# Two rooms instead of one for the value pairs of a mixer layer, each pair loaded one tile earlier

## The chip, the cores and the metric

The kernel runs on one core of one Trainium2 chip. The metric is the device time of one execution in microseconds (us); below 0.3% of it (about 3.8 us) a difference counts as none. The profile is one execution taken by the hardware profiler. Engines are named as in it: PE (matrix multiply), PEld (its weight loads), DVE (vector), ACT (scalar), POOL, and SP, which only issues transfers; "ACTq" and the like is the engine's sequencer, for instance when it issues a transfer (DMA).

## The reference

One layer over 1024 tokens of 1024 channels, in float32. What matters here:

```python
h = rmsnorm(x, g_pre_mix)
proj = h @ w_in                              # u_pool (512) | q (512) | k (512) | v (512)
y_pool = multiscale_pool(u_pool, ...) @ w_br_pool     # 4 groups, trailing means over 2, 4, 8, 16 tokens
o_sb = stick_breaking_attention(q, k, v)              # 8 heads of 64, strictly causal
gates = sigmoid(h @ w_gate + b_gate)
x = x + rmsnorm((g_pool * y_pool + g_sb * (o_sb @ w_br_sb)) @ w_out, g_post_mix)
h2 = rmsnorm(x, g_pre_mlp)
x = x + rmsnorm(relu(h2 @ w_up)**2 @ w_down, g_post_mlp)
```

The kernel's attention needs, in place of v, the difference of each token's v row and the next one's ("value pairs").

## The kernel before, in words

**Precision and tiling.** Each float32 matrix is split into a high and a low part, and each product is three matmuls (`mm3`, L110 to L112) of 128x128 by 128x512. The stages follow each other: input and v, then `phase_project` (q, k and gates), then attention, merge and MLP. The change touches only what runs beside `phase_project`.

**The products.** `phase_project` handles twelve pairs of column blocks (`PAIRS`, L499): pairs 0 to 4 are gates, 5 to 8 are q, k, q, k, and 9 to 11 gates. Each pair is seven half products (a Strassen scheme), numbered here c = 0 to 83, so that pair i has c = 7i to 7i+6; each is 12 matmuls into a PSUM bank. `newbank` (L666) deals seven banks out of three pools in turn: "d" (2 banks), "z" (2), "at" (3). So product c shares its bank with c+6 in the first two pools and with c+9 in the third; `later` takes four such banks too, all before c = 30. The bank is read by DVE or ACT into the parts u, c11, v and c22 (L693 to L717); u has two buffers, each other part one.

**The sixteen staged results.** Of a pair, products 2, 5, 6 and 7 complete the results c11, c22, v and u (L695, L712, L716, L718). For the gates a result is squashed in place and stored. For q and k (`result`, L548 to L558) it is split by ACT (L550) and DVE (L551) into a staged tile, which POOL's queue stores in two or four transfers of 256 KB (L556, and L558 for q alone). Call these S1 to S16: S1 to S4 are c11, c22, v and u of pair 5, and so on to S16, u of pair 8. Their tiles take turns between two rooms (`staged`, L537): S1 in m1, S2 in m0, S3 in m1 and so on, odd ones in m1, even ones in m0.

**The rooms.** Pool `mx` has four rooms m0 to m3 of 4 KB per partition, one buffer each: a new tile in a room waits until the one before it has been read and, if it is stored, until its store has landed.

**The background.** `later` (L560) is a generator. One step of it runs inside each product, before the product's own result is dealt with (L679), and a second one at twelve of the products 6 to 33 (L681). Its step numbers, from 0, are used below; from product 34 on, step s runs inside product c = s - 13, and so before the result of that product asks for its room.

- Steps 9 to 42: pooling of four groups g. Group g loads u (m0 or m3 in turn, L568), makes g+1 running sums in m1 and m2 in turn (L590), the difference (L595 to L599), its high and low parts ph and pq (L603, L604), the matmuls, two scaled results (L611, L612) that overwrite the last sum and u, and stores both to `yscr` (L619). For g = 3 the matmuls are in step 40 and the stores in step 41; pq is in m0, ph in m1, the last sum in m2, u in m3.
- Steps 43 to 84: eight value tiles t. Tile t loads its pair p on ACT's queue (two transfers, L626) in step 43, 49, 55, 61, 67, 73, 77, 81, and three steps later subtracts (DVE, L631), splits (ACT L634, DVE L635) into v, and stores v to `sscr` (POOL, L636). The room of p is m2, and of v m3; for t = 5 and 7 it is m0 and m1.

**Behind the stage** attention's first head is loaded into m2 and m3 (L724) and the second into m0 and m1 (L748, L781 to L787), both on SP's queue, with the second half of the pooling result behind the second head.

**The order on each engine** is made at compile time by a list scheduler: it takes a later instruction ahead of one whose operands or room it expects later. On the chip each engine then runs its list in that order.

Of the kernel before, what the change touches and what calls it, by code (L numbers as in the profile page):

```python
# [19 lines left out]
F32 = mybir.dt.float32  # L20
# [12 lines left out]
P = 128  # L33
H = 512
NK = 8
# [17 lines left out]
class Block:  # L53
# [506 lines left out]
    def later(self, newbank):  # L560

        nc = self.nc
        def whole(n, dt=F32, name="ps"):
            return self.mx.tile([P, 1024], dt, name=name, tag=f"m{n}")

        def u_load(g):
            u = whole(3 * (g % 2), name="u")
            nc.scalar.dma_start(u, self.uscr[g])  # L568
            return u

        nxt_u = u_load(0)
        wm = whole(1)[:, :512].rearrange("p (g n) -> p g n", g=4)
        nc.scalar.dma_start(wm, self.wmix)
        for _ in range(6):
            yield
        yield
        yield
        wmh, wml = (self.rp.tile([P, 4, P], F32R, name=f"wm{n}", tag=f"rb{n}") for n in range(2))
        nc.scalar.copy(wmh, wm)
        nc.vector.tensor_sub(wml, wm, wmh.bitcast(F32))  # L580
        yield
        for g in range(4):
            iu = 3 * (g % 2)
            u = nxt_u
            cur, n = u, 0
            for i in range(g + 1):
                sh = 1 << i
                n = 1 + i % 2
                nxt = whole(n, name="win")
                nc.vector.tensor_add(nxt[:, sh:], cur[:, sh:], cur[:, : 1024 - sh])  # L590
                nc.vector.tensor_copy(nxt[:, :sh], cur[:, :sh])
                cur = nxt
                yield
            w = 1 << (g + 1)
            nc.vector.scalar_tensor_tensor(  # L595
                out=cur[:, w:], in0=cur[:, w:], scalar=1.0 / w, in1=u[:, w:], op0=ALU.mult, op1=ALU.subtract
            )
            nc.vector.tensor_mul(cur[:, :w], cur[:, :w], self.rcnt[:, :w])
            nc.vector.tensor_sub(cur[:, :w], cur[:, :w], u[:, :w])  # L599
            yield  # L600
            sc = self.vt[:, V_PSC + g : V_PSC + g + 1]
            ph, pq = whole(3 - n, F32R, "ph"), whole(3 - iu, F32R, "pq")
            nc.scalar.copy(ph, cur)  # L603
            nc.vector.tensor_sub(pq, cur, ph.bitcast(F32))  # L604
            yield
            yield
            ds = [self.zps.tile([P, H], F32, name="dm", tag="o", bufs=1), newbank()]
            for h, d in enumerate(ds):
                c = slice(h * H, h * H + H)
                self.mm3(d, [(wmh[:, g, :], wml[:, g, :], ph[:, c], pq[:, c])])  # L610
                nc.scalar.activation(cur[:, c].bitcast(F32R), d, AF.Copy, scale=sc)  # L611
                nc.vector.scalar_tensor_tensor(  # L612
                    out=u[:, c].bitcast(F32R), in0=d, scalar=sc, in1=cur[:, c], op0=ALU.mult, op1=ALU.subtract
                )
            if g < 3:
                nxt_u = u_load(g + 1)
            yield
            for t, scr in zip((cur, u), self.yscr):
                nc.gpsimd.dma_start(scr[:, g, :], t)  # L619
            yield  # L620
            yield
        for t in range(NK):
            n = 0 if t in (5, 7) else 2
            p = self.mx.tile([P, 2, H], F32, name="vpair", tag=f"m{n}")
            for j in range(2):
                nc.scalar.dma_start(p[:, j, :], self.vscr[t * P + j : t * P + j + P, :])  # L626
            yield
            yield
            yield
            e = p[:, 0, :]  # L630
            nc.vector.tensor_sub(e, e, p[:, 1, :])  # L631
            e = e.rearrange("p (h x) -> p h x", h=8)
            v = self.mx.tile([P, 8, P], F32R, name="vs", tag=f"m{n + 1}")
            nc.scalar.copy(v[:, :, 0:64], e)  # L634
            nc.vector.tensor_sub(v[:, :, 64:128], e, v[:, :, 0:64].bitcast(F32))  # L635
            nc.gpsimd.dma_start(self.sscr[t], v.rearrange("p h x -> p (h x)").bitcast(F32))  # L636
            yield
            if t < 5:
                yield
                yield  # L640
# [1033 lines left out]
```

## Time and profile before

| | |
|---|---|
| median of 3 runs | 1263.16 us (1262.45 to 1266.2) |
| the profiled execution | 1262.18 us, span 1260.4 us, mean granted PE clock 0.998 |
| DVE, ACT, POOL busy | 77%, 50%, 14% of the span |
| `phase_project` in the trace | about 105 to 336 us from the span's start |
| DMA | 283.27 MB, 225 GB/s mean |

In the views quoted below a row of a timeline reads: start, duration, engine, line, operation, output<-inputs, shapes, count, and in square brackets how long the engine had been idle and what ended it. Rows of windows give the busy time of each engine (with its number of instructions), the granted clock ("PEclk", 1.00 is full) and the DMA share. A step of the chain of waits is start, duration, what.

### The profile page before, as it was taken

Reading aid. Unit: us, or ns where it says so; the run is one execution under the profiler, and the core shown is the slowest. Engines: PE = TensorE matmul, PEld = TensorE weight load, DVE = VectorE, ACT = ScalarE, POOL = GpSimd, SP = SyncE. Lnnn points to the kernel's source line nnn. Section 1 sums busy time; section 2 is a strip of 40 time slices with the busy share of each in tenths; the row PEclk is TensorE's granted clock in tenths of the full one; section 3 lists DMA queues with packets and bytes.
Section 4 is the critical chain, followed back from the end, with each engine's and each line's share of the span. In section 5 each row is a group of like instructions: output and inputs, shape, how many; then the busy total and the mean of one; then the engine's idle time right before and its main releaser. Section 6 shows DMA issues by size and latency. Waiting matters only on the chain.

```text
span 1260.4 us, 16197 instructions
## 1 busy us (share of the span) xinstructions
PE 1238.4 (98%) x5707; PEld 1021.2 (81%) x5707; DVE 968.6 (77%) x1311; ACT 631.9 (50%) x1010; POOL 180.0 (14%) x320
## 2 busy tenths in 40 slices
PE   9999999999999999999999999999999999999998
PEld 6887788788787887878788888888888888888887
DVE  8849886786488998778797879878854655776975
ACT  7237543344266576663566645554554433344352
POOL 2212111442001101110110012221121100001000
PEclk9999999999999999999999999999999999999999
DMA  6586896987998665446657577665559996557552
GB/s 225 168 232 177 241 275 155 317 298 240 320 358 334 204 184 150 101 137 215 225 161 242 195 268 264 235 224 200 183 198 340 300 305 228 185 194 252 202 190 68
DMA packets 110497, 283.27 MB, mean 225 GB/s; under 512 B 12496, under 2 KB 17744, under 8 KB 109264
## 3 DMA queue, kind: packets, MB, share of 16 engines
q1 hardware_dynamic: 65840, 165.41, 37.6%
q0 software_dynamic: 31040, 91.26, 25.2%
q10 hardware_dynamic: 13536, 25.57, 6.2%
q8 instruction: 45, 0.74, 0.2%
q14 instruction: 36, 0.29, 0.1%
HBM read 208.65 MB, written 94.50 MB: 241 GB/s over the span
## 4 chain that ended last, share of the span: by engine, by line
PE 72%; DMA 9%; issue 8%; DVE 7%; ACT 2%; POOL 1%; ACTq 0%; SPq 0%; DVEq 0%; POOLq 0%
PE d L112 17%; PE d L110 17%; PE d L111 17%; PE o L853 2%; PE dbr L108 2%; PE dbr L111 2%; PE dbr L112 2%; DMA qscr<-ks 2%; PE at L829 2%; DMA vpair<-vscr 1%; DVE T L816 1%; PE sw L110 1%; DMA vscr<-ev 1%; PE sw L112 1%; PE sw L111 1%
## 5 line engine op out<-in xcount | busy, mean ns | idle before, releaser
L111 PE MATMUL d<-blo,whi 128*128 128x512 f32 (+1 forms) x456 | 172.3, 378 | 0.0
L112 PE MATMUL d<-bhi,wlo 128*128 128x512 f32 (+1 forms) x456 | 171.9, 378 | 0.0
L110 PE MATMUL d<-bhi,whi 128*128 128x512 f32 (+1 forms) x456 | 168.7, 378 | 0.0
L112 PEld LDWEIGHTS d<-bhi,wlo 128*128 128x128 f32 x456 | 85.8, 188 | 16.1
L111 PEld LDWEIGHTS d<-blo,whi 128*128 128x128 f32 x456 | 85.7, 188 | 16.0
L110 PEld LDWEIGHTS d<-bhi,whi 128*128 128x128 f32 x456 | 85.5, 188 | 15.9
L816 DVE TENSOR_TENSOR_SCAN T<-T,past 128x512 f32<-128x512 f32 (+3 forms) x64 | 85.0, 1346 | 4.9 <-ACT T L814 4.5
L111 PE MATMUL d<-b_lo,whi 128*128 128x512 f32 x196 | 76.2, 390 | 0.5 <-DVE b_lo L1100 0.5
L110 PE MATMUL d<-b_hi,whi 128*128 128x512 f32 x196 | 75.7, 390 | 0.0
L112 PE MATMUL d<-b_hi,wlo 128*128 128x512 f32 x196 | 74.2, 389 | 0.0
L78 DVE TENSOR_TENSOR wlo<-wraw,whi 128x1024 fp32r<-128x1024 f32 x45 | 54.9, 1220 | 13.9 <-ACT whi L76 12.3
L76 ACT CAST whi<-wraw 128x1024 fp32r<-128x1024 f32 x45 | 47.5, 1055 | 36.0 <-PE d L111 20.1
L1395 ACT CAST whi<-slots_hi 128x1024 fp32r<-128x1024 f32 x29 | 30.5, 1053 | 68.8 <-PE d L111 62.6
L1397 DVE TENSOR_TENSOR wlo<-slots_hi,whi 128x1024 fp32r<-128x1024 f32 x29 | 35.5, 1224 | 38.2 <-ACT whi L1395 38.2
L814 ACT ACTIVATE T<-z 128x256 f32<-128x256 f32 (+2 forms) x96 | 45.2, 493 | 35.1 <-PE z L812 31.2
L1395 ACT CAST whi<-slots_lo 128x1024 fp32r<-128x1024 f32 x27 | 28.4, 1053 | 62.3 <-PE d L111 52.1
L110 PE MATMUL sw<-h_hi,whi 128*128 128x512 f32 x144 | 56.9, 395 | 2.1 <-DVE c L694 2.1
L111 PE MATMUL sw<-h_lo,whi 128*128 128x512 f32 x144 | 56.6, 393 | 0.0
L112 PE MATMUL sw<-h_hi,wlo 128*128 128x512 f32 x144 | 56.2, 393 | 0.0
L839 ACT CAST ahi<-at 128x512 fp32r<-128x512 f32 (+1 forms) x96 | 44.1, 484 | 22.3 <-PE at L829 20.0
L840 DVE TENSOR_TENSOR alo<-at,ahi 128x512 fp32r<-128x512 f32 (+1 forms) x96 | 49.9, 541 | 6.7 <-ACT ahi L839 6.6
L1397 DVE TENSOR_TENSOR wlo<-slots_lo,whi 128x1024 fp32r<-128x1024 f32 x27 | 33.0, 1222 | 26.0 <-ACT whi L1395 25.9
(438 smaller groups left out, 3444.9 us busy)
## 6 DMA issues: line engine op xcount, KB each, us to landing
wraw<-w SPq DMA_DIRECT2D x53, 512.0 KB, 4.9
ext_b<-ascr SPq DMA_DIRECT2D x40, 512.0 KB, 6.9
wscr<-w POOLq DMA_DIRECT2D x32, 512.0 KB, 9.4
slots_hi<-w SPq DMA_DIRECT2D x10, 1024.0 KB, 7.9
slots_lo<-w SPq DMA_DIRECT2D x10, 1024.0 KB, 8.8
qq<-qscr SPq DMA_DIRECT2D x32, 256.0 KB, 5.2
pscr<-p SPq DMA_DIRECT2D x32, 256.0 KB, 3.0
u<-pscr ACTq DMA_DIRECT2D x32, 256.0 KB, 4.5
```

Source lines behind the costliest of these rows:

```text
L76: nc.scalar.copy(hi, raw)
L78: self.lows.append(nc.vector.tensor_sub(lo, raw, hi.bitcast(F32)).ins)
L108: nc.tensor.matmul(ps, wh, rh, start=first and i == 0, stop=False)
L110: nc.tensor.matmul(ps, wh, rh, start=first and i == 0, stop=False)
L111: nc.tensor.matmul(ps, wh, rl, start=False, stop=False)
L112: self.last_mm = nc.tensor.matmul(ps, wl, rh, start=False, stop=last and i == n - 1).ins
L814: self.after = nc.scalar.activation(f, z[:, :n], AF.Sigmoid, scale=-1.0)
L816: nc.vector.tensor_tensor_scan(f[:, ::-1], f[:, ::-1], past[:, ::-1], 1.0, ALU.mult, ALU.max)
L839: self.att_hi = nc.scalar.copy(hi[:, c:], at[:, c:]).ins
L840: self.att_lo = nc.vector.tensor_sub(lo[:, c:], at[:, c:], hi[:, c:].bitcast(F32)).ins
L1395: last_split[0] = nc.scalar.copy(hi, src).ins
L1397: last_split[1] = nc.vector.tensor_sub(lo, src, hi.bitcast(F32)).ins
```

## The change

The value pairs t = 0, 2, 4, 6 use m2 and m3, and t = 1, 3, 5, 7 use m0 and m1. Each pair is loaded a tile ahead: the load of t = 0 moves to step 40, behind the last pooling matmuls, and the loads of t = 1 to 7 move to steps 44, 50, 56, 62, 68, 74 and 78; the subtraction, the split and the store stay in steps 46, 52, 58, 64, 70, 76, 80 and 84. In the pooling groups 0 and 3 the running sums begin in m2 instead of m1, so that the last sum of group 0 is in m2 and that of group 3 in m1, and their ph in the other one.

```diff
+        def v_load(t):
+            p = self.mx.tile([P, 2, H], F32, name="vpair", tag=f"m{2 - 2 * (t % 2)}")
+            for j in range(2):
+                nc.scalar.dma_start(p[:, j, :], self.vscr[t * P + j : t * P + j + P, :])
+            return p
...
-                n = 1 + i % 2
+                n = 1 + (i + (g in (0, 3))) % 2
...
             if g < 3:
                 nxt_u = u_load(g + 1)
+            else:
+                nxt_p = v_load(0)
             yield
...
         for t in range(NK):
-            n = 0 if t in (5, 7) else 2
-            p = self.mx.tile([P, 2, H], F32, name="vpair", tag=f"m{n}")
-            for j in range(2):
-                nc.scalar.dma_start(p[:, j, :], self.vscr[t * P + j : t * P + j + P, :])
+            n = 2 - 2 * (t % 2)
+            p = nxt_p
             yield
+            if t < NK - 1:
+                nxt_p = v_load(t + 1)
             yield
             yield
             e = p[:, 0, :]
```

## The prediction

> **What bounds the kernel now.** I read the page first, then PE's windows of 10 us, then the waits that ended PE's gaps there, then the lists of ACT and DVE between 200 and 320 us.
>
> ```profile
> span 1260.4 us, 16197 instructions
> ...
> PE 1238.4 (98%) x5707; PEld 1021.2 (81%) x5707; DVE 968.6 (77%) x1311; ACT 631.9 (50%) x1010; POOL 180.0 (14%) x320
> ```
>
> PE is busy 98% of the span, so a change can only pay where PE stops, and can only cost where it makes PE stop. Windows beside the background generator (columns: window, length, then busy time and count of PE, PEld, DVE, ACT, POOL, then clock, DMA share, GB/s):
>
> ```profile
> 180.00:190.00 10.00, 10.00 (x46) 8.29 (x45) 7.00 (x12) 4.08 (x7) 0.08 (x1) 1.00 0.67 257
> 210.00:220.00 10.00, 9.81 (x44) 7.81 (x43) 4.01 (x6) 4.56 (x6) 1.50 (x2) 1.00 1.10 289
> 220.00:230.00 10.00, 7.87 (x28) 6.04 (x27) 7.37 (x12) 1.82 (x3) 3.23 (x6) 0.83 0.82 276
> 230.00:240.00 10.00, 10.00 (x46) 8.29 (x45) 7.61 (x11) 3.79 (x6) 3.13 (x7) 1.00 1.01 358
> ```
>
> A full window holds 46 matmuls, so one matmul takes 0.22 us and a product (12 of them) 2.7 us. The window 220 to 230 holds 28: 18 are missing, 3.9 us, and 2 more in the window before, 0.4 us. The clock of 0.83 is (1 - 0.83) x 10 = 1.7 us of it, the rest is PE standing still. The chain of waits through that place, and PE's rows that ended a gap:
>
> ```profile
> 205.23 8.40 DMA yscr<-win
> ...
> 214.01 9.10 DMA vpair<-vscr
> ...
> 223.23 0.06 DVE vpair L631
> ...
> 223.84 0.69 DVE c L694
> ...
> 224.57 0.79 PE sw L110
> ```
>
> ```profile
> 218.73 0.50 PE L110 MATMUL sw<-h_hi,s1hi 128*128 128x512 f32 x1 [0.19 <-ACT u L693]
> ...
> 224.57 0.79 PE L110 MATMUL sw<-h_hi,whi 128*128 128x512 f32 x1 [2.13 <-DVE c L694]
> ```
>
> The store of the last pooling sum (room m2) takes 8.40 us; only then can the first value pair be loaded into m2, 9.10 us; DVE holds at its subtraction (L631); behind it in DVE's list stands the c11 of pair 5 (L694), and PE waits 2.13 us for that. The two gaps also show how far PE gets without DVE and ACT. The u and c11 of pair 5 are products 35 and 36, so PE stood at products 41 and 42, which share their banks: six products on.
>
> **How a room is handed on.** This decides the case. In m0 stand, by the program text before: pq of group 3, S2, S4 and so on to S12, then p of t = 5 (called p5, its split result v5), S14, S16, p7; in m1: ph, S1, S3 to S15, v5, v7.
>
> ```profile
> 203.98 0.68 ACT L611 ACTIVATE win<-sw,vt 128x512 fp32r<-128x512 f32 x1
> ...
> 229.41 0.63 ACT L550 ACTIVATE qs<-c 128x512 fp32r<-128x512 f32 x1 [4.23 <-DVE c L710]
> ```
>
> From 203.98, when the last pooling product is read and with it pq is done, to 229.41, when S2 is written, m0 is empty. p5 needs nothing but the room, for its data are old; its load is the row at 290.74 below. So a room is handed on in the order of the text, even if a later tenant is ready and the room empty. Here is what it costs when p5 then comes between S12 and S14 (ACT's list, then DVE's):
>
> ```profile
> 267.74 0.63 ACT L550 ACTIVATE qs<-c 128x512 fp32r<-128x512 f32 x1 [0.38 <-DMA qscr<-ks]
> 268.94 0.63 ACT L550 ACTIVATE qs<-c 128x512 fp32r<-128x512 f32 x1 [0.58 <-DMA qscr<-ks]
> ...
> 277.27 0.63 ACT L550 ACTIVATE qs<-v 128x512 fp32r<-128x512 f32 x1 [1.47 <-DMA qscr<-qs]
> ...
> 279.27 0.63 ACT L550 ACTIVATE qs<-u 128x512 fp32r<-128x512 f32 x1
> 288.29 0.63 ACT L550 ACTIVATE ks<-c 128x512 fp32r<-128x512 f32 x1 [8.39 <-DMA qscr<-qs]
> ...
> 290.74 1.08 ACTq L626 DMA_DIRECT2D vpair<-vscr  x2
> ...
> 294.99 0.63 ACT L550 ACTIVATE ks<-v 128x512 fp32r<-128x512 f32 x1 [0.98 <-DMA qscr<-ks]
> ...
> 301.64 0.62 ACT L634 CAST vs<-vpair 128x512 fp32r<-128x512 f32 x1 [5.07 <-DMA qscr<-ks]
> ...
> 303.02 0.63 ACT L550 ACTIVATE ks<-c 128x512 fp32r<-128x512 f32 x1 [0.23 <-DVE vs L635]
> ...
> 309.88 0.63 ACT L550 ACTIVATE ks<-u 128x512 fp32r<-128x512 f32 x1 [1.75 <-DMA qscr<-ks]
> ...
> 312.53 0.58 ACT L693 COPY u<-sw 128x512 f32<-128x512 f32 x1
> ...
> 316.01 0.81 ACTq L626 DMA_DIRECT2D vpair<-vscr  x2
> ```
>
> ```profile
> 280.12 0.69 DVE L710 TENSOR_TENSOR c<-v,sw 128x512 f32<-128x512 f32 x1
> ...
> 302.29 0.69 DVE L635 TENSOR_TENSOR vs<-vpair,vs 128x512 fp32r<-128x512 f32 x1 [2.96 <-ACT vs L634]
> ...
> 303.68 0.69 DVE L551 SCALAR_TENSOR_TENSOR ks<-c,ks 128x512 fp32r<-128x512 f32 x1
> ...
> 304.89 0.68 DVE L710 TENSOR_TENSOR c<-v,sw 128x512 f32<-128x512 f32 x1
> ```
>
> The rows are S9 (267.74), S10, S11, S12 (279.27), S13 (288.29), p5's load (290.74), S15 (294.99), v5 (301.64), S14 (303.02), S16 (309.88), the u of pair 10 (312.53), p7's load. S14 holds c22 of pair 8, complete at 280.12, and gets m0 only at 303.02, because p5 leaves m0 when v5 is split, and v5 must wait for S15's store in m1: 5.07 us of waiting on ACT. The next c22 (pair 9, L710 at 304.89) runs straight behind DVE's read of S14 (303.68): a staged result that waits keeps its part, and the part keeps a PSUM bank. PE doesn't feel it here. From the same rows a room is held 10.6 us by a q result (9.53, 10.33, 11.02, 11.47) and 6.6 us by a k result (6.70, 6.65, 6.86, 6.13).
>
> **The change part by part.**
>
> *First pair early.* In step 40 its room m2 holds ph of group 3, free at 203.98. Its load then lands before 215, and DVE no longer holds at L631. Next late is v0's room m3: u of group 3, stored beside the last sum, which landed at 213.6 (205.23 + 8.40). ACT may hold there as it now holds for the load, so the 0.4 us may stay. I take -4.0 us; the bounds are -4.3 (all of the gap) and -2 (half stays). The clock's share rests on the row of 220 to 230: 2.13 us of standing cost 1.7 us of clock. [...]
>
> *Pooling sums.* Group 3, and group 1 likewise, waits for the store of the sum before:
>
> ```profile
> 185.99 1.22 DVE L590 TENSOR_TENSOR win<-u 128x1023 f32<-128x1023 f32 x1 [3.00 <-DMA yscr<-win]
> ```
>
> These 3.00 us of DVE go. PE holds 46 matmuls in 180 to 190, so its banks cover them: I cost this at nothing, and the same if they stay. Groups 0 and 3 only swap rooms.
>
> *Issues.* Sixteen load issues stay sixteen, earlier in ACT's list:
>
> ```profile
> L626 ACTq DMA_DIRECT2D vpair<-vscr x16: 326/378/1465, 213.7 to 316.4; - x16
> L631 DVE TENSOR_TENSOR vpair<-vpair x8: 684/692/692, 223.2 to 320.2; 128x512 f32<-128x512 f32 x8
> ...
> DMA to landing us min/median/max: 2.6/4.4/9.1
> ```
>
> Each is 0.38 us of ACT's sequencer; ACT is 50% busy: nothing. A load takes 4.4 us (2.6 to 9.1), and a subtraction 0.69.
>
> *Odd pairs in m0 and m1.* By the text the order becomes, in m0: p1, S2, S4, p3, S6, S8, S10, p5, S12, S14, S16, p7; in m1: S1, v1, S3, S5, S7, S9, v3, S11, S13, S15, v5, v7. For p1 the new order costs little: v1 follows S1. But p3 (step 56) sits in m0 ahead of S6, S8, S10, and v3 (step 64) comes behind S9, a result of the next pair; for p5, v5 comes behind S15. Each odd pair now holds m0 for eight steps of the text instead of three.
>
> Worked out from the times of before. S9's store frees m1 at 277.27 (there S11 took it). v3 takes it: 0.62 + 0.69, and p3 leaves m0 at 278.6. Only now S6 (c22 of pair 6) is split, 0.63 + 0.69, to 279.9, and DVE can write c22 of pair 7 (0.69), to 280.6. That is product 53, and product 59 needs its bank. PE's product 42 began at 224.57, so 59 would begin at 224.57 + 1.7 + 17 x 2.7 = 272.2, now 4.0 earlier, 268.2. Ahead of it the scheduler can take 60, 61 and 64, whose banks come free without S6 and S8: 8.1 us, to 276.3. **Stop of 4.3 us** to 280.6; 59 ends at 283.3. Then 62 needs the bank of 56, u of pair 8, whose part is held by S8: m0 at 278.6 + 6.6 = 285.2, split to 286.5, L693 (0.58) to 287.1. **Stop of 3.8.**
>
> Further: S10 takes m0 at 291.8, p5 at 302.4, landed at 306.8. In m1, v3 is stored:
>
> ```profile
> L636 POOL DMA_DIRECT2D sscr<-vs x8: 571/580/588, 227.9 to 322.6; - x8
> ...
> DMA to landing us min/median/max: 3.6/5.8/8.9
> ```
>
> 1.3 + 0.6 + 5.8 = 7.7, so S11 at 285.0, S13 at 295.6, S15 at 302.2, v5 at 308.8. p5 leaves at 310.1, S12 (u of pair 7) is split to 311.4, u of pair 9 copied to 312.0. That is product 63, bank of 69. PE has from 287.1 the products 62, 63, 65 to 68 and 70, 18.9 us, and 1.7 of low clock, to 307.7. **Stop of 4.3.** Low clock after it: 1.7.
>
> Sum: -4.0 + 4.3 + 3.8 + 1.7 + 4.3 + 1.7 = **+11.8 us**. The profiled execution took 1262.18, so 1274.0; the median of the runs lies 1.0 above it: **1275**.
>
> The ends: if S9 comes 4 us earlier with the gain, and rooms are held 9.5 and 6.1 us, the last stop ends 6.1 us earlier (4, and 1.1 + 0.5 + 0.5 from the rooms), and with the clock staying up another 3.4 go: +2. At the upper end the stage's exit is late too:
>
> ```profile
> 332.03 0.32 SPq L787 DMA_DIRECT2D kk<-qscr  x1
> ```
>
> The second head's k waits in m1's queue behind v7, at 332.03, 4 us before the products end at about 336. By the room times above v7's store lands at about 347, 1 us before a products' end of 348: up to 3 us more. And where ACT's list holds in full on one room as at 288.29 (8.39 us, unfelt now for lack of a full bank queue), that adds up to 8.4: +23.
>
> **The rivals.**
>
> *The rooms are not handed on by the text* (or the list finds another way): odd pairs slip into gaps, only the gain is left, -4.0: 1259. For it: 25 us of empty m0 at 203.98. Against it: p5 did not take them. [...] Chance 0.15.
>
> *The queue is there, but PE covers it*: the scheduler, which knows the rooms, draws more products forward, or stores land faster with less traffic. The stops shrink from 12.4 us to 4 or so: 1260 to 1266, say 1263. For it: S14's 23 us cost PE nothing. Against it: then one c22 was late and none of the u that PE ran into. Chance 0.13.
>
> *Worse*: ACT and DVE hold in list order while S6 and S12 wait, and the weight splits behind them come late too: 1283 to 1290, decided by whether a hold on ACT exceeds the 8.39 us that PE tolerated. Chance 0.10.
>
> **How the numbers follow.** The forecast, on the side of slower, has 0.62; its own range is 1265 to 1286. 0.3% is 3.8 us, about what a measurement of this kernel can tell from nothing. Faster by more: two thirds of the first rival and a little of the second, 0.13. Within: the rest of the first and most of the second, 0.15. Slower: 0.72. The range takes in the first rival's centre and the forecast's upper end: 1259 to 1287.
>
> **What would show it.** Right: no gap at 222 us; vpair loads of t = 0 and 1 at about 204; between the split of v3 and a late S6 more than 30 us after its result was added (product 46 ends at 268.2 - 12 x 2.7 = 235.8); PE waiting for L710 near 275 to 281, then for L693 near 285 and 310, with the clock below 1.00 there; `phase_project` ending some 12 us later. Wrong: S6 at about 250 as now, all windows from 230 to 340 as full as that of 230 to 240; then the rooms went by readiness, and only the gap at 222 counts.

## The result and the profile after

The changed kernel takes 1279.63 us (median of five runs, 1274.91 to 1280.39) against 1262.72 us before (five runs, 1261.85 to 1266.2): 1.012 times as long, with a 95% interval of 1.0107 to 1.0132. It is slower by 17 us. The profiled execution is the quickest of the five, 1274.91 us with a span of 1273.2; the other four spans are 1277.0 to 1278.7, and no trace shows where those 3.8 to 5.5 us went. What follows explains the profiled one, 12.7 us longer than the profiled one of before.

The page after (span, busy time and share per engine):

```profile
span 1273.2 us, 16176 instructions
PE 1239.6 (97%) x5707; PEld 1022.3 (80%) x5707; DVE 970.1 (76%) x1311; ACT 632.6 (50%) x1010; POOL 179.9 (14%) x320
```

No engine has more work: DVE has 1.5 us more and ACT 0.7, and the bytes moved are the same 283.27 MB. The time was lost waiting. The two longest waits of PE from 200 to 380 us (line that waited, releaser: total, times, longest), and windows there:

```profile
PE sw L110 <- DVE u L719: 10.8, 1, 10.8
PE sw L110 <- DVE v L716: 1.9, 1, 1.9
```

```profile
220.00:230.00 10.00, 10.00 (x46) 8.28 (x45) 6.63 (x10) 2.69 (x4) 3.75 (x7) 1.00 1.06 352
...
240.00:250.00 10.00, 8.15 (x36) 6.41 (x35) 6.27 (x11) 1.89 (x3) 3.99 (x8) 1.00 0.98 372
...
270.00:280.00 10.00, 2.26 (x10) 1.53 (x9) 5.11 (x7) 2.29 (x4) 2.24 (x4) 0.76 0.69 218
280.00:290.00 10.00, 6.92 (x19) 5.47 (x20) 6.17 (x10) 2.48 (x4) 5.20 (x9) 0.56 0.68 200
```

The window of 220 to 230, which held 28 matmuls, is full: the old gap is gone. In its place stand a short gap near 248 and one long stop near 280, after which the granted clock is low (0.56 from 280 to 290). (The changed kernel's lines are 6 to 8 higher: the splits of a value tile are L642 and L643, the c22 of a pair is written at L718 and the same product is added to u at L719, the copy of u is L701.)

How far PE lags at equal work is seen best when the k-th matmul record of one trace is set against the k-th of the other. First column: time in the profile of before; then the matmuls done by then, and how much later the changed kernel did the next one (negative is earlier):

```
before at   matmuls   after later by
  100         417        0.01 us
  140         582        1.26
  220         933        0.78
  230         959       -3.18
  250        1047       -1.05
  280        1180       12.76
  350        1483       12.46
 1000        4491       12.84
```

Three terms and a gain: +1.3 us before 140, -4.0 at the old gap, +2.1 near 248, +13.8 at the long stop. Their sum is 13.2 (with 0.5 won back before 220, 12.8), and after 280 the lag stays between 12 and 15 us.

**The long stop.** (S1 to S16, m0 to m3, p and v are named as in the text ahead of the prediction; "the text" below is the order of the program.) First what came before it: DVE adds the c22 of pair 6, which S6 is to stage, and subtracts in p3; then ACT's issue of p3's load, and S7.

```profile
248.64 0.68 DVE L718 TENSOR_TENSOR c<-v,sw 128x512 f32<-128x512 f32 x1
...
263.63 0.69 DVE L639 TENSOR_TENSOR vpair<-vpair 128x512 f32<-128x512 f32 x1 [2.36 <-DMA vpair<-vscr]
```

```profile
255.60 0.81 ACTq L574 DMA_DIRECT2D vpair<-vscr  x2
...
266.48 0.63 ACT L550 ACTIVATE ks<-v 128x512 fp32r<-128x512 f32 x1 [7.38 <-DMA qscr<-ks]
```

S6's result is complete at 249.3. Its room m0 comes free at 255.4, when the store of S4 has landed, and p3 takes it at 255.60, as in the text. p3 is ready for its split at 264.3, but S7 and then S9 take m1 ahead of v3, again as in the text. Then ACT's list (S9, v3, S6, S8 and the copy of u behind it), DVE's, and PE's row:

```profile
272.57 0.63 ACT L550 ACTIVATE qs<-c 128x512 fp32r<-128x512 f32 x1 [2.04 <-DMA qscr<-ks]
...
278.89 0.62 ACT L642 CAST vs<-vpair 128x512 fp32r<-128x512 f32 x1 [5.18 <-DMA qscr<-qs]
280.27 0.63 ACT L550 ACTIVATE ks<-c 128x512 fp32r<-128x512 f32 x1 [0.76 <-DVE vs L643]
...
286.51 0.63 ACT L550 ACTIVATE ks<-u 128x512 fp32r<-128x512 f32 x1 [2.03 <-DMA qscr<-ks]
287.90 0.59 ACT L701 COPY u<-sw 128x512 f32<-128x512 f32 x1 [0.76 <-DVE ks L551]
```

```profile
275.29 0.69 DVE L529 TENSOR_TENSOR wraw<-wraw 128x512 f32<-128x512 f32 x1
279.54 0.69 DVE L643 TENSOR_TENSOR vs<-vpair,vs 128x512 fp32r<-128x512 f32 x1 [3.56 <-ACT vs L642]
280.93 0.69 DVE L551 SCALAR_TENSOR_TENSOR ks<-c,ks 128x512 fp32r<-128x512 f32 x1 [0.69 <-ACT ks L550]
281.65 0.69 DVE L718 TENSOR_TENSOR c<-v,sw 128x512 f32<-128x512 f32 x1
282.26 0.68 DVE L719 TENSOR_TENSOR u<-u,sw 128x512 f32<-128x512 f32 x1
282.86 0.68 DVE L723 TENSOR_TENSOR v<-v,sw 128x512 f32<-128x512 f32 x1
283.45 0.68 DVE L725 TENSOR_TENSOR u<-u,sw 128x512 f32<-128x512 f32 x1
```

```profile
269.38 0.39 PE L110 MATMUL sw<-ht_hi,a0hi 128*128 128x512 f32 x1
...
283.08 0.77 PE L110 MATMUL sw<-ht_hi,whi 128*128 128x512 f32 x1 [10.82 <-DVE u L719]
```

Read upward from the bottom: PE needs the bank of the product that L718 and L719 read. L718 writes c22 of pair 7 into the part that S6 (the c22 of pair 6) still holds; S6 needs room m0; p3 sits in m0 until v3 is split; v3 needs m1, which the store of S9 leaves just before 278.89. S9 is a result of the next pair (7). Each link follows the one before within 0.2 us. And in DVE's list L723 and L725, whose products were long in their banks, stand behind L718: DVE idles 3.56 us, and these two banks stay full as well. (The row at 269.38 is product 61, which PE's list has ahead of 59; 59 is the one that waits to 283.08.)

### The profile page after: what moved, and what is told of

Read it like the earlier page. It is cut to its first block, busy times and chain, and to the rows that moved or that the text cites. A ratio compares the mean times of both kernels' runs of the same rounds, so it can differ in the third digit from the quotient of the medians.

```text
span 1273.2 us, 16176 instructions
## 1 busy us (share of the span) xinstructions
PE 1239.6 (97%) x5707; PEld 1022.3 (80%) x5707; DVE 970.1 (76%) x1311; ACT 632.6 (50%) x1010; POOL 179.9 (14%) x320
## 2 busy tenths in 40 slices
DMA packets 110498, 283.27 MB, mean 222 GB/s; under 512 B 12497, under 2 KB 17745, under 8 KB 109265
## 4 chain that ended last, share of the span: by engine, by line
PE 67%; DVE 5%; DMA 5%; ACT 2%; issue 2%; POOL 0%; ACTq 0%; SPq 0%; DVEq 0%; POOLq 0%
PE d L112 18%; PE d L111 18%; PE d L110 18%; PE o L861 2%; PE dbr L111 2%; PE dbr L112 2%; PE dbr L108 2%; PE at L837 2%; DMA qscr<-ks 2%; DVE T L824 1%; PE z L817 1%; PE z L820 1%; DMA sscr<-vs 1%; DMA gt<-gscr 1%; DMA vpair<-vscr 1%
## 5 line engine op out<-in xcount | busy, mean ns | idle before, releaser
L112 PEld LDWEIGHTS d<-bhi,wlo 128*128 128x128 f32 x456 | 85.8, 188 | 15.8
L78 DVE TENSOR_TENSOR wlo<-wraw,whi 128x1024 fp32r<-128x1024 f32 x45 | 54.9, 1220 | 16.2 <-ACT whi L76 14.7
```

The costliest lines, as they stand in the source:

```text
L78: self.lows.append(nc.vector.tensor_sub(lo, raw, hi.bitcast(F32)).ins)
L112: self.last_mm = nc.tensor.matmul(ps, wl, rh, start=False, stop=last and i == n - 1).ins
```

## The experiments

**Theory.** A room goes to its tenants in the order of the program text. With p3 put into m0 between S4 and S6, and v3 into m1 behind S9, S6 cannot begin before S9 is stored; the held c22 then keeps its PSUM bank full, and PE stops. **Rivals.** (a) The earlier transfers themselves cost: they meet the stores and weight loads. (b) It is p3 alone, and the rest of the change is harmless. (c) The new order of the pooling sums costs.

Each kernel below is the changed one with the edit shown, unless said otherwise. An edit also changes the lists that the scheduler makes, so two kernels can differ in more than the room named; each is read from its own rows. The lag of PE against before at equal work, as in the table above (us; the columns stand in the order in which the kernels are told; what differs at 100 lies ahead of all that the edits touch, and is to be taken off):

```
before   p3      no p3 in    pairs in   late    pooling     first    all in   all in m2,
at       alone   m0, m1      new rooms  loads   sums only   load     m2       group 3 only
100      0.41      2.49       0.86       1.76     0.04       0.06     1.13      0.40
140      1.65      4.07       1.70       2.78     1.40       0.88     2.04      0.18
220      1.35      3.59       1.22       2.30     0.92       0.40     1.64     -0.30
230     -2.61     -0.37      -2.74      -1.66    -2.89      -2.61    -2.32     -4.26
250     -2.61      1.24      -2.74      -0.15    -2.88      -2.59    -2.32     -4.26
280      6.69      1.34      -2.38      -0.14    -2.88      -2.59    -2.32     -4.26
300      6.69      1.34       2.63       5.12    -2.88      -2.59    -1.32     -4.26
310      6.69     10.20       2.63       5.12    -2.24      -2.25    -1.22     -4.26
330      6.69     10.20       2.63       5.53     4.20       4.27    -1.22     -4.26
350     10.81     10.16       1.42      10.23     3.47       3.04    -2.88     -5.92
370      13.53     13.55       5.87      13.84     3.69       3.40    -2.97     -6.03
1000     15.81     13.22       4.55      13.92     4.25       5.51    -1.89     -4.59
```

### p3 alone in the other rooms

Only t = 3 (and 7, which was there before) uses m0 and m1; t = 1 and 5 go to m2 and m3.

```diff
-            p = self.mx.tile([P, 2, H], F32, name="vpair", tag=f"m{2 - 2 * (t % 2)}")
+            p = self.mx.tile([P, 2, H], F32, name="vpair", tag=f"m{0 if t in (3, 7) else 2}")
...
-            n = 2 - 2 * (t % 2)
+            n = 0 if t in (3, 7) else 2
```

> The whole change, but t = 1 and t = 5 go to m2 and m3, so that of the pairs that come among S1 to S16 only t = 3 is in m0. Room-order theory: the long stop near 270 to 283 us stays, waiting for the part c22 or u behind S6 and S8, 8 to 12 us; no stop near 310 from p5: 1268 to 1276 us. Rival (it is p1 that started the lateness): no long stop, 1260 to 1264 us.

One run: 1278.22 us (before beside it 1263.32, median of 14), above the 1268 to 1276 expected. The chain is the changed kernel's, 6 us earlier: v3, S6, PE.

```profile
272.93 0.62 ACT L642 CAST vs<-vpair 128x512 fp32r<-128x512 f32 x1 [0.98 <-DMA qscr<-qs]
274.30 0.63 ACT L550 ACTIVATE ks<-c 128x512 fp32r<-128x512 f32 x1 [0.76 <-DVE vs L643]
...
277.12 0.76 PE L110 MATMUL sw<-ht_hi,whi 128*128 128x512 f32 x1 [6.43 <-DVE u L719]
```

The gap of 6.43 us and the low clock behind it (0.79 from 270 to 280, 0.87 from 280 to 290) make 9.3 us (-2.61 to 6.69). So p3 alone is enough for a stop of this kind. But another 6.8 us came at the stage's exit (6.69 to 13.53 at 370), and the whole delay is about that of the changed kernel.

### All but p3

```diff
-            p = self.mx.tile([P, 2, H], F32, name="vpair", tag=f"m{2 - 2 * (t % 2)}")
+            p = self.mx.tile([P, 2, H], F32, name="vpair", tag=f"m{0 if t in (1, 5, 7) else 2}")
...
-            n = 2 - 2 * (t % 2)
+            n = 0 if t in (1, 5, 7) else 2
```

> The whole change, but the pair t = 3 and its split result go to m2 and m3 as before. Room-order theory: p1 and p5 alone are left in m0, so the stop near 272 goes; p5 ahead of S12 may still stop PE near 310 by up to 5 us: 1259 to 1266 us. Rival (early loads): one of seven less, 1273 to 1278.

1279.81 us (1275.23 to 1285.79, four runs), ratio 1.014 (1.0106 to 1.0174); the expectation was missed. The stop near 280 is gone, but the next one is there: v5, S12 (u of pair 7), then PE waiting for the copy of u that needs its part.

```profile
303.65 0.62 ACT L642 CAST vs<-vpair 128x512 fp32r<-128x512 f32 x1 [4.34 <-DMA qscr<-ks]
305.02 0.63 ACT L550 ACTIVATE qs<-u 128x512 fp32r<-128x512 f32 x1 [0.24 <-DVE vs L643]
...
307.59 0.80 PE L110 MATMUL sw<-h_hi,s1hi 128*128 128x512 f32 x1 [5.75 <-ACT u L701]
```

That is 8.9 us with the low clock (0.84 from 300 to 310, 0.82 from 310 to 320; 1.34 to 10.20), for the tenant and the part that the prediction named for its third stop. In the changed kernel it didn't appear: there PE came 13 us late. Rival (b) falls: take one stop away and PE reaches the next, and by 370 the lag is 13.55 (11.1 of it since 100), not far below the changed kernel's 14.44.

### The odd pairs in rooms of their own

The whole change, loads as early as in it, but p of odd t in two half-size rooms of another pool; v stays in m1.

```diff
+            if t % 2:
+                p = [self.rp.tile([P, H], F32, name="vpair", tag=f"rb{j}") for j in range(2)]
+            else:
+                b = self.mx.tile([P, 2, H], F32, name="vpair", tag="m2")
+                p = [b[:, j, :] for j in range(2)]
...
-            e = p[:, 0, :]
-            nc.vector.tensor_sub(e, e, p[:, 1, :])
+            e = p[0]
+            nc.vector.tensor_sub(e, e, p[1])
```

> The whole change, but the odd pairs are loaded into two half rooms of another pool that nobody else uses at that time; their split results stay in m1. Loads are as early as in the change. Room-order theory: S6 no longer waits for v3, so the stop of 10.8 us near 272 goes: 1258 to 1264 us, S6 before 258 us. Rival (early loads cost by themselves): 1275 or more, as with the change.

1267.22 us (1266.79 to 1270.74, four runs), ratio 1.0044 (1.0027 to 1.006): 3.7 us above before instead of 17, with the transfers as early, though also above the 1258 to 1264 expected. S6 now runs as soon as its c22 is added (at 250.83; m0 had been free since 247.45, when the store of S4 landed), 29 us before its time in the changed kernel, and the window 270 to 280 is full. One stop is left, in the room that p still shares through v: v3 stands in m1 ahead of S11 (the v of pair 7), and PE waits for the v after it (5.0 us with the clock, 0.83 from 290 to 300; -2.38 to 2.63).

```profile
250.87 0.63 ACT L550 ACTIVATE ks<-c 128x512 fp32r<-128x512 f32 x1 [0.83 <-DVE c L722]
...
282.09 0.62 ACT L646 CAST vs<-vpair 128x512 fp32r<-128x512 f32 x1
...
290.36 0.62 ACT L550 ACTIVATE qs<-v 128x512 fp32r<-128x512 f32 x1
...
293.09 0.56 PE L110 MATMUL sw<-ht_hi,s1hi 128*128 128x512 f32 x1 [3.13 <-DVE v L720]
```

Rival (a) falls: early transfers without the shared room don't make the stop at 280.

### Odd pairs in m0 and m1, but loaded in the old steps

```diff
-            p = nxt_p
+            p = nxt_p if t == 0 else v_load(t)
             yield
-            if t < NK - 1:
-                nxt_p = v_load(t + 1)
```

> The whole change, but the pairs t = 1 to 7 are loaded in their old number of steps before use (three), so that p3 asks for m0 after S6 and ahead of S8. Room-order theory: S6 goes at its time (before 258 us), S8 waits for v3 instead and with it u of pair 8; a stop of 2 to 6 us in place of 10.8: 1260 to 1268 us. Rival (early loads): nothing but the first load is early, so 1259 us with no stop at all.

1277.6 us (1276.2 to 1280.25, four runs), ratio 1.0127 (1.0108 to 1.0145), above what was expected. p3 now asks for m0 five steps later, behind S6, and S6 runs at 257.18. But S8 is behind p3, and PE waits for the u that needs S8's part:

```profile
280.57 0.62 ACT L640 CAST vs<-vpair 128x512 fp32r<-128x512 f32 x1 [7.01 <-DMA qscr<-qs]
282.04 0.63 ACT L550 ACTIVATE ks<-u 128x512 fp32r<-128x512 f32 x1
...
284.67 0.50 PE L110 MATMUL sw<-h_hi,s0hi 128*128 128x512 f32 x1 [3.35 <-ACT u L699]
```

5.3 us here (-0.15 to 5.12), and 8.3 more at the exit (5.53 to 13.84 at 370). In these two kernels the early load decides which staged result stands behind the pair, and makes little difference to how much is lost.

### Only the pooling sums

The kernel before with one edit:

```diff
-                n = 1 + i % 2
+                n = 1 + (i + (g in (0, 3))) % 2
```

> Only the swapped rooms of the pooling sums (groups 0 and 3) on the kernel before. Looked at for PE's progress at equal matmul counts: +1.3 us at 140 us if the new pooling order is the cause of the early loss, 0 as the prediction had it. Since group 3's last sum is then in m1, the first pair's load into m2 no longer waits for a store, so the gap at 222 shrinks too: 1260 to 1264 us.

One run: 1266.41 us, above what was expected. Two things show. First, the gap at 222 is gone (0.92 to -2.89) although every load stands in its old step: with the last sum of group 3 in m1, m2 holds only ph, which no store has to leave; the first pair's load is issued at 204.35. Moving the first load to step 40 isn't what wins. Second, PE has two new gaps early on (1.21 us at 113 and 1.28 at 127), and two more at 311 and 330:

```profile
311.29 0.50 PE L110 MATMUL sw<-h_hi,whi 128*128 128x512 f32 x1 [2.15 <-DVE v L715]
330.08 0.47 PE L110 MATMUL sw<-ht_hi,whi 128*128 128x512 f32 x1 [2.14 <-DVE u L711]
```

### The first load and the pooling sums, all else as before

The changed kernel with tags of before and the loads of t = 1 to 7 in their old steps: the `p = nxt_p if t == 0 else v_load(t)` edit above, and `0 if t in (5, 7) else 2` in the tag and in n.

> Of the change only the first value pair's early load and the swapped rooms of the pooling sums; all other pairs are loaded in their old steps into their old rooms (m2, and m0 for t = 5 and 7). Room-order theory: the gap at 222 us goes and none of the new stops comes, so 1258.7 us (1257 to 1261), S6 near 250 us. Rival, that moving loads forward costs by itself (traffic, ACT's queue): the one moved load already costs something, 1263 or more.

1265.88 us (1263.62 to 1268.71, ten runs), ratio 1.0024 (1.0013 to 1.0035): the expected gain is missing; the 2.4 us more are below what counts as a difference. The 3.0 us won at 222 (0.40 to -2.61) are kept until 300 and lost between 300 and 330, 6.9 us. The first stop has p5 behind it, which before already held S14 up (in m0: S12, p5, S14); its c22 of pair 9 ran at 304.89 before and runs at 308.64 here, and PE comes 2.6 us earlier for it. Why the queue itself is later here is not shown. The second has p7 behind it: DVE holds in its list for the load, and the c22 and u that PE needs stand behind that subtraction.

```profile
306.76 0.63 ACT L550 ACTIVATE ks<-c 128x512 fp32r<-128x512 f32 x1 [0.24 <-DVE vs L641]
...
311.17 0.50 PE L110 MATMUL sw<-h_hi,whi 128*128 128x512 f32 x1 [2.04 <-DVE v L721]
330.11 0.77 PE L110 MATMUL sw<-ht_hi,whi 128*128 128x512 f32 x1 [2.33 <-DVE u L717]
```

```profile
326.70 0.69 DVE L637 TENSOR_TENSOR vpair<-vpair 128x512 f32<-128x512 f32 x1 [5.99 <-DMA vpair<-vscr]
```

So with no new pair in m0 at all, a gain upstream is given back: the two value pairs that before has in these rooms were bearable only at the times that PE and the queue had before.

### All pairs in m2 and m3

If that is so, the gain stays once p5 and p7 leave m0 too. The kernel of the last experiment with 2 for every t:

```diff
-            n = 0 if t in (5, 7) else 2
+            n = 2
```

> The first pair's early load and the swapped pooling rooms, and all eight pairs in m2 and m3, loaded in their old steps; no value tile in m0 or m1. Theory now: the tenants of m0 and m1 are a chain that PE cannot outrun, in the kernel before just as in the changed one; e2 lost its gain there at p5 (stops near 311 and 330 us). Without p5, v5, p7 and v7 that chain is about 20 us shorter, so the gain at 222 us stays: 1260 us (1258 to 1262), no stop of PE from 230 to 335 us, S16 split before 302 us. Rival (the early load or the new pooling order costs later on its own): 1264 to 1267 as e2.

1259.87 us (1259.47 to 1263.29, ten runs), ratio 0.9978 (0.9969 to 0.9987): 3.5 us less, as expected, and just under what counts as a difference. S14 runs at 295.01 instead of 306.76, and one gap of 0.7 us, at 296, is all that PE has between 130 and 350.

### The same, with only group 3's sums begun in m2

```diff
-                n = 1 + (i + (g in (0, 3))) % 2
+                n = 1 + (i + (g == 3)) % 2
```

> As e7_all_in_m2, but only pooling group 3 swaps its rooms, group 0 not. If the 1.3 us lost near 110 to 130 us in all kernels with the new pooling order come from group 0's earlier first sum, they go: 1258.7 us, 1.3 below e7_all_in_m2, with PE at 140 us within 0.5 us of the kernel before at equal matmul counts. If they come from elsewhere: equal to e7_all_in_m2.

1257.58 us (1256.97 to 1258.36, five runs), ratio 0.9954 (0.994 to 0.9967): faster than both kernels. S16, which ran at 313.59 with p5 and p7 in m0, runs at 295.38, and the place of the long stop is full:

```profile
270.00:280.00 10.00, 10.00 (x46) 8.27 (x45) 6.45 (x9) 5.14 (x7) 3.88 (x7) 1.00 0.85 261
280.00:290.00 10.00, 10.00 (x46) 8.29 (x45) 8.68 (x14) 2.36 (x4) 2.96 (x5) 1.00 0.83 289
```

From 100 to 140 PE here wins 0.2 us on before, where the kernels with group 0's sums moved lose 0.8 to 1.6: rival (c) is true of group 0, for that much of the 17 us.

## Why the prediction was right or wrong

**Direction and the hand-over of the rooms held; the nearness of the size is in part luck.** 1275 was forecast and 1279.63 measured. By the medians the change is 17 us; the profiled executions, of which the changed kernel's is the quickest of its five, differ by 12.7 where the sum said 11.8. The cause is the forecast's: rooms handed on by the text, p3 in m0 until v3 gets m1 behind S9. v3 came at 278.89 (forecast 277.27), S6 at 280.27 (278.6), c22 of pair 7 at 281.65 (279.9). Of the signs that were named, the loads at 204, the late S6 (31 us after its result was added) and the stop near 280 came; the two stops at L693 did not. The likeliest rival, in which the pairs slip into gaps and -4.0 us is left, is excluded: it has S6 at about 250, and S6, complete 6 us before p3 took m0, still ran behind p3; with p elsewhere it ran at 250.87, straight behind the addition. (That S7 and S9 passed v3 doesn't tell the two apart: their results were complete at 251.7 and 257.1, before p3 was ready for its split.) The second room of the pairs was shared with the staged results, and the trace is 12.7 us longer.

In the sum, the stops and the low clock behind them were 15.8 us, and 13.8 were seen; the two terms that it put at nothing or little were 3.4 (1.3 and 2.1). With the gain 0.4 larger these errors nearly cancel: 12.8 against 11.8.

**The gain: -4.0 forecast, -4.4 seen** (1.26 to 0.78 before 220, then to -3.18). The whole gap went, with the 0.4 us before 220 that the step let stay. What brings it is not what the step said. ACT held for v0's room until u's store landed, as foreseen, and nobody was late for it; but the experiment on the sums alone shows that group 3's swap gives this gain without the early load.

**Pooling sums "at nothing": wrong, +1.3 us.** The step looked at a DVE wait that goes, and not at where the freed instruction would be put. In before, group 0's first sum stood behind two splits that PE needs; in the changed kernel, whose list has it no longer wait for m1, it is 4 us earlier, ahead of them. First before, then after, then two gaps that PE has only with it:

```profile
111.62 0.69 DVE L1100 TENSOR_TENSOR ht_lo<-x,ht_hi 128x512 fp32r<-128x512 f32 x1
...
113.36 1.22 DVE L590 TENSOR_TENSOR win<-u 128x1023 f32<-128x1023 f32 x1
```

```profile
109.24 1.22 DVE L596 TENSOR_TENSOR win<-u 128x1023 f32<-128x1023 f32 x1
...
112.24 0.69 DVE L1108 TENSOR_TENSOR ht_lo<-x,ht_hi 128x512 fp32r<-128x512 f32 x1
```

```profile
112.98 0.50 PE L111 MATMUL sw<-ht_lo,a0hi 128*128 128x512 f32 x1 [1.16 <-DVE ht_lo L1108]
127.02 0.50 PE L110 MATMUL sw<-ht_hi,whi 128*128 128x512 f32 x1 [1.27 <-ACT whi L1216]
```

Every kernel with group 0's swap has both gaps, and the one without it has neither. That the second gap, on a weight split, comes from the same move is only argued.

**p1 "costs little": +2.1 us near 248.** ACT's row of v4, then PE's:

```profile
244.37 0.62 ACT L642 CAST vs<-vpair 128x512 fp32r<-128x512 f32 x1 [5.84 <-DVE vpair L639]
```

```profile
248.17 0.50 PE L110 MATMUL sw<-ht_hi,s1hi 128*128 128x512 f32 x1 [1.85 <-DVE v L716]
```

With t = 1 and 3 out of m2 and m3, v4 comes early, and ACT holds 5.84 us for its pair with S3 behind it (245.08; 238.87 in before), whose part the v of pair 6 needs. S3 could not have run sooner anyway: v1 now stands in m1 between S1 and S3, and by the trace its store lands at 245.06. In the kernel with late loads the row of S3 names such a store:

```profile
246.45 0.64 ACT L550 ACTIVATE qs<-v 128x512 fp32r<-128x512 f32 x1 [0.57 <-DMA sscr<-vs]
```

The gap is there in the three kernels in which p1 sits in m0 (1.85, 1.33 and 1.22 us) and in no other. The kernel with rooms of their own has v1 in m1 too, the same hold on ACT, S3 at 247.00 and no gap: its PE list has products 52 and 55 ahead of 51, the one that needs this v. So the step was wrong in that v1 follows S1 but S3 must follow v1; what p in m0 itself adds was not separated.

**The stops: 4.3, 3.8 and 4.3 forecast, one of 10.82 seen.** The first is 6.5 us longer than forecast. The step had PE take products 60, 61 and 64 ahead while 59 waited, 8.1 us, to 276.3. PE took 61 alone (269.38 to 272.26) and stopped. By the order in which banks are dealt, 60 and 64 need the banks of 54 and 55, which DVE's L723 and L725 read, and these stood behind the held L718; the bank of 61 is read by L716, which ran at 268.36. The forecast counted the banks and not the order on the engine that frees them. Against that, 59's own turn was misread: 272.2 in the working, but in the profile of before it begins at 270.42 (43 is one of the 17 products counted behind 42, and PE had run most of it before 42), and in the changed kernel it would have come at 269.38, where 61 stands; the forecast had 268.2. So it drew 5.2 us less ahead from a start 1.2 us later, and stopped 4.0 us earlier than forecast; the other 2.5 are the end, 283.08 against 280.6 (v3 later by 1.6, and L719 behind L718). The second stop then didn't come: the copy of u ran at 287.90 (forecast 287.1), when PE had those put-off products to do. Nor did the third: u's copy behind S12 ran at 311.12 (forecast 312.0), but PE, 13 us late, did not need its bank yet. The experiment without p3 shows it to be real, 5.75 us, where PE is in time for it.

**The clock.** 1.7 us after each of two stops was forecast; behind the one of 10.82 us it was 3.0 (13.8 less 10.82). In the experiments gaps of 6.43 and 5.75 us cost 2.9 and 3.1 beside themselves, and gaps of 3.35 and 3.13 cost 1.9 (lag gained, less the gap). The last section sets gaps beside the clock.

**The exit, kept for the upper end, seems to fix the size.** The row of SP's queue after (the second head's k, which waits for v7 to leave m1; 332.03 before):

```profile
345.31 0.32 SPq L795 DMA_DIRECT2D kk<-qscr  x1
```

The forecast let this wait add up to 3 us to the stops. It is no addition. When the same load is issued, against the lag of PE at 370 (us):

```
                       k of head 2 at   later than before   PE's lag at 370
after                     345.31             13.3               14.4
p3 alone                  345.49             13.5               13.5
no p3 in m0, m1           344.62             12.6               13.6
late loads                346.76             14.7               13.8
pairs in new rooms        332.86              0.8                5.9
first load                335.15              3.1                3.4
pooling sums only         335.66              3.6                3.7
all in m2                 321.56            -10.5               -3.0
all in m2, group 3 only   319.37            -12.7               -6.0
```

In the four kernels that put more odd pairs through m0 and m1, or other ones, the queue of tenants ends 12.6 to 14.7 us later, and PE is 13.5 to 14.4 us late behind it, whether it paid in one stop (after: 12.76 already at 330), later (without p3: 10.20 at 330, 3.4 at the exit) or mostly at the exit (late loads: 8.3). Without what each had at 100 us the pairs are 13.3 and 14.4, 13.1 and 13.1, 10.1 and 11.1, 13.0 and 12.1. Part of what PE waits for at the exit is named: ylo and yhi, loaded behind the second head (1.41 us in p3 alone, 1.45 and 0.5 in late loads, where from 355.33 to 359.81 the 128x512 matmuls also start 0.43 us apart instead of 0.23). That the exit would have cost the changed kernel the same without its long stop is argued from these rows; no run had the late end of the queue alone. So the near agreement of 11.8 with 12.7 is in part luck: the stops were added up one by one, and what they amount to is the lateness of the queue's end, which the working had (v7's store at about 347, for a k loaded before at 332) and did not read as the size.

**What the sum left out** is that the stage has little slack to give: with no pair added to m0 and m1, a PE that is 3 us early, and a queue some 4 us later, already stop at p5 and p7.

## What to carry to other kernels

When a buffer is given to one more user, write down the order in which its tenants get it, and for each the tenant of another buffer that it must wait for: loading ahead into a shared buffer holds it for longer, and two such buffers can chain a result to one of the next block; in these runs the end of that queue told more of the cost than the first stop that it caused. Take the gain of a removed gap only after asking what PE meets when it comes that much earlier; here it stayed only once the shared rooms were relieved. And an operation that loses a wait moves up in its engine's list (here from 113.36 to 109.24), which can delay what PE needs more than it helps.

## What the runs showed that was not expected

In these runs the length of a gap alone does not tell whether the clock falls. In the kernel with the pooling sums alone, the gap of 2.15 us at 311 left it at 1.00 and that of 2.14 us at 330 did not:

```profile
310.00:320.00 10.00, 8.71 (x38) 7.20 (x39) 7.26 (x11) 5.43 (x8) 1.17 (x2) 1.00 0.63 179
...
330.00:340.00 10.00, 9.92 (x37) 8.02 (x38) 4.77 (x6) 3.69 (x6) 2.20 (x4) 0.83 0.92 321
```

A clock of 0.83 over 10 us is 1.7 us, the same as behind the 2.13 us before. Single gaps of PE beside the granted clock in the 10 us around their end:

```
kernel               gap ends at   PE idle   granted clock
after                  248.17        1.85    1.00 (240 to 250)
first load             311.17        2.04    1.00 (310 to 320)
pooling sums only      311.29        2.15    1.00 (310 to 320)
before                 224.57        2.13    0.83 (220 to 230)
pooling sums only      330.08        2.14    0.83 (330 to 340)
first load             330.11        2.33    0.83 (330 to 340)
pairs in new rooms     293.09        3.13    0.83 (290 to 300)
```

What sets the second and the third row apart from the fourth and the fifth is not shown. The seven gaps are of 1.85 to 3.13 us; the four with a low clock lost 1.7 us each by it. Behind the stop of 10.82 us the clock was 0.51 from 283 to 289, 2.9 us, near the 3.0 above. So in these traces gaps of 2.13 to 3.35 us, where the clock fell, cost 1.7 to 1.9 us on top, and those of 5.75, 6.43 and 10.82 us some 3.
